# A two-layer decoder trunk on one core: first half of each output product finished in pairs, eight load slots, modulation tiles three ahead

## The chip, the core and the metric

One core of a Trainium2 chip. The time is device microseconds of one execution. The kernel before was run three times: median 2452.31 us, 2449.97 to 2458.36. The engines: TensorE (PE in the profile, its weight loads PEld), VectorE (DVE), ScalarE (ACT), GpSimd (POOL), and SyncE (SP), whose queue issues nearly all loads.

## What is computed

x is one sequence of 256 tokens and 2048 features, c one conditioning vector of 2048. All numbers are float32. Two layers; layer 0 mixes tokens with chunked gated linear attention (GLA), layer 1 with softmax attention that has a forget gate (FoX). Each mixer is followed by a gated MLP with a causal convolution of width 3. Cut to its frame:

```python
cond = jax.nn.silu(c)
for i in range(DEPTH):
    mod = (cond @ w_mod[i] + b_mod[i])[:, None, :]
    sh_m, sc_m, g_m, sh_f, sc_f, g_f = jnp.split(mod, 6, axis=-1)
    h = rmsnorm(x, norm_mix[i]) * (1.0 + sc_m) + sh_m
    y = gla_mixer(h, ...) if i % N_MIXERS == 0 else fox_mixer(h, ...)
    x = x + (1.0 + g_m) * y
    h = rmsnorm(x, norm_ffn[i]) * (1.0 + sc_f) + sh_f
    x = x + (1.0 + g_f) * conv_ffn(h, ffn_w_up[i], ...)
return rmsnorm(x, norm_final)
```

Each mixer ends in a product with w_out (2048 x 2048) and each MLP in a product with ffn_w_down (5632 x 2048). These are the four output products. w_mod (2 x 2048 x 12288) is read once, for one vector: the modulation.

## The kernel before

**Products.** Features lie on the 128 partitions, tokens along the free side. A weight tile is 128 rows by 1024 columns, 512 KB. Each float32 product is made of three matmuls on split operands: weight high by input high, weight high by input low, weight low by input high (lines 612 to 614 in stream_a, 648 to 650 in stream_b, where the weights are the moving operand). ACT makes the high half of a weight tile (wh, line 117), DVE the low half (wl, line 121); there are four buffers of each (AHEAD + 1). stream_a runs over the weight tiles k of one group of 1024 output columns, and for each k over its eight 128-column pieces m: 24 matmuls a tile, added up in four PSUM banks, two pieces to a bank. The pool psA has six banks.

**Loads.** All weight tiles stand in one list (plan) in the order of use. next_w (line 561) hands out the next tile and has split_to (line 571) split up to three tiles beyond it, or fewer where hold says so, and issue loads for up to RING - 1 = 6 tiles beyond those that are split. A load takes one of RING = 7 slots of one pool (ringt, line 100), and is issued on SP's queue; it stays there until a slot is free, and what is behind it stays too.

**Modulation.** mod_tasks (line 236) makes a task for each 128 x 1024 tile of w_mod: a load into a slot of the same ring (line 250), and a product with one column of cond added to an accumulator by DVE (line 271, the first one line 269). At the end of 1024 columns the accumulator is transposed and reduced (lines 283 and 284, or line 304 with line 313) and PE adds up the rest (line 300 or 293). These tasks are spread as background work: after each weight tile tick (line 368) first fills the row of loaded tasks (prefetch, line 350) up to PEND = 2, and then runs as many tasks as pace says; set_pace (line 396) divides the tasks that remain by a number of ticks (N1 = 26 for the last of them in the GLA output product, others for other stages). Small steps of other work (side) are spread in the same way.

**Order.** The instructions are traced in the order of the program. From that a scheduler makes the order of each engine, by what is ready first in its own model of time; so work further on in the program can go ahead on an engine. On the chip each engine then keeps that order. Line 119 and others pin one step behind another.

**Output products.** add_residual (line 678) calls stream_a twice, for columns 0 to 1023 and 1024 to 2047. The first call runs all tiles, and behind it the four residual steps are written, one for each bank: residual (line 667) has two DVE steps that add the scaled bank to x (line 671) and the square for the next norm (stat, lines 454, 462 and 473). The second call gets the residual as done: its last TAIL = 3 tiles are held, without a tick, and then multiplied piece by piece; after each second piece, when a bank is complete, its residual step follows. After the second call come the sum over features for the norm (line 483), what was deferred of the modulation (line 293), and the next h (lines 527 to 530).

Of the kernel before, what the change touches and what calls it, by code (L numbers as in the profile page):

```python
# [28 lines left out]
GH = 4  # L29
FH = 16  # L30
SECT = {"sh_m": 0, "sc_m": 1, "g_m": 2, "sh_f": 3, "sc_f": 4, "g_f": 5}
RING = 7
AHEAD = 3
DIRECT = 4
XAFTER = 1
# [2 lines left out]
BACK = 1  # L38
STAGE = 3
FREE = 0  # L40
PEND = 2
BLOCKS = (8, 8)
FIRST = (6, 0)
SLOW = 0.0
TAIL = 3
# [25 lines left out]
def kernel(  # L71
# [10 lines left out]
    const = ctx.enter_context(tc.tile_pool(name="const", bufs=1))  # L82
    ring = ctx.enter_context(tc.tile_pool(name="ring", bufs=RING))
    big = ctx.enter_context(tc.tile_pool(name="big", bufs=NBIG))
# [15 lines left out]
    def ringt(shape, s="w"):  # L100
        return ring.tile(shape, F32, tag="w", name=nm(s))
# [10 lines left out]
    def split_w(src, moving, after=None):  # L112
        n_ = src.shape[-1]
        o1, o2 = (0, 0) if moving else HELD
        hi = tmp.tile([P, WCOLS], F32R, tag="wh", bufs=AHEAD + 1, name=nm("wh"))[:, o1:o1 + n_]
        lo = tmp.tile([P, WCOLS], F32R, tag="wl", bufs=AHEAD + 1, name=nm("wl"))[:, o2:o2 + n_]
        nc.scalar.copy(out=hi, in_=src)  # L117
        with ExitStack() as es:
            if after is not None:
                es.enter_context(tc.issue_after(after))  # L120
            order["v"] = nc.vector.tensor_tensor(out=lo, in0=src, in1=hi.bitcast(F32), op=ALU.subtract).ins  # L121
        return hi, lo
# [101 lines left out]
    deferred = []  # L224
# [4 lines left out]
    def after_startup(on=True):  # L229
        es = ExitStack()  # L230
        if on and startup["left"] > 0 and len(startup["loads"]) >= BACK:
            startup["left"] -= 1
            es.enter_context(tc.issue_after(startup["loads"][-BACK]))
        return es
# [108 lines left out]
    def modcol(l, key, m):  # L343
        return mod[:, l * 6 + SECT[key], m:m + 1]
# [5 lines left out]
    def prefetch(depth):  # L350
        while bg and len(pending) < depth:
            load, f = bg.popleft()
            load()
            pending.append(f)
# [6 lines left out]
    def flush_resting(all_=False):  # L361

        for r in resting:
            r[0] -= 1
        while resting and (all_ or resting[0][0] <= 0):
            resting.popleft()[1]()

    def tick():
        prefetch(PEND)
        flush_resting()  # L370
        with ExitStack() as es:
            for key in ORDERED:
                if order[key] is not None and fetched["use"] > FREE:
                    es.enter_context(tc.issue_after(order[key]))
            steps()
# [185 lines left out]
    def next_w(kt, cols, hold=None):  # L561
        i = fetched["use"]
        assert plan[i][1] == kt and plan[i][3] == tuple(cols), (plan[i][1:], kt, cols)
        fetched["use"] += 1
        run, look = AHEAD if hold is None else hold, RING - 1
        if i < STAGE:
            run, look = min(run, STAGE - i), 1
        split_to(min(i + 1 + run, len(plan)), look)
        return splits.popleft()

    def split_to(end, look=RING - 1):
        while fetched["split"] < end:
            while fetched["load"] < min(fetched["split"] + look, len(plan)):
                w_, kt_, nk_, cols_, mov_ = plan[fetched["load"]]
                fetched["load"] += 1
                wt = ringt([P, 1024])
                o = 0
                for c0, cn in cols_:
                    if nk_ == 1:
                        with after_startup():  # L580
                            nc.sync.dma_start(out=wt[:, o:o + cn], in_=w_[kt_ * P:(kt_ + 1) * P, c0:c0 + cn])
                        o += cn
                    else:
                        nc.sync.dma_start(out=wt[:, :nk_ * cn].rearrange("p (k r) -> p k r", r=cn),
                                          in_=w_[kt_ * P:(kt_ + nk_) * P, c0:c0 + cn]
                                          .rearrange("(k p) r -> p k r", p=P))
                        nc.vector.memset(wt[:, nk_ * cn:nk_ * cn + P - cn], 0.0)
                        o = nk_ * cn + P - cn
                raws.append((wt[:, :o], mov_))
            with ExitStack() as es:  # L590
                after = None
                if gate["n"] > 0:

                    gate["n"] -= 1
                    es.enter_context(tc.issue_after(gate["early"] if gate["n"] > 0 else gate["late"][0]))
                    after = gate["late"][1]
                splits.append(split_w(*raws.popleft(), after))
            fetched["split"] += 1

    def banks():  # L600
        return [psA.tile([P, 2, T], F32, tag="a", name=nm("pa")) for _ in range(4)]

    def stream_a(kts, cols, rhs, done=None):

        ps = banks()
        held = []

        def mms(m, k, wh, wl, rh, rl):
            first, last = k == kts[0], k == kts[-1]
            ms = slice(m * P, (m + 1) * P)  # L610
            o = ps[m // 2][:, m % 2, :]
            nc.tensor.matmul(o, wh[:, ms], rh, start=(first and m % 2 == 0), stop=False, skip_group_check=True)  # L612
            nc.tensor.matmul(o, wh[:, ms], rl, start=False, stop=False, skip_group_check=True)  # L613
            nc.tensor.matmul(o, wl[:, ms], rh, start=False, stop=last, skip_group_check=True)  # L614

        for k in kts:
            rh, rl = rhs(k)
            tail = done is not None and k in kts[-TAIL:]
            wh, wl = next_w(k, cols, kts[-1] - k + 1 if tail else None)
            if tail:  # L620
                held.append((k, wh, wl, rh, rl))
                continue
            for m in range(8):
                mms(m, k, wh, wl, rh, rl)
            tick()
        if done is not None:
            split_to(min(fetched["use"] + 1, len(plan)))
            if len(deferred) > 1:
                deferred.pop(0)()
            for m in range(8):  # L630
                for args in held:
                    mms(m, *args)
                if m % 2 == 1:
                    done(m // 2, ps)
        return ps
# [31 lines left out]
    def residual(l, key, m0):  # L667
        def done(pair, ps):
            for j in range(2):
                m = m0 + 2 * pair + j  # L670
                nc.vector.scalar_tensor_tensor(out=xT[:, m, :], in0=ps[pair][:, j, :], scalar=modcol(l, key, m),
                                               in1=xT[:, m, :], op0=ALU.mult, op1=ALU.add)
            stat(m0 + 2 * pair, m0 > 0)
            if fin and m0 and 0 < pair < 3:
                transpose_out(m0 + 2 * pair - 2, 2)
        return done

    def add_residual(l, key, kts, rhs):
        ps = stream_a(kts, [(0, 1024)], rhs)
        for pair in range(4):  # L680
            residual(l, key, 0)(pair, ps)
        if l == 1 and key == "g_f":
            prepare_out()
        stream_a(kts, [(1024, 1024)], rhs, residual(l, key, 8))
# [11 lines left out]
    def gla(l, h):  # L696
# [3 lines left out]
        def piece(key, kts, c0):  # L700
            if key == "a":
                return narrow(kts, c0, RANK, h)
            if key[0] == "v":
                return stream_b(kts, c0, h)
            return [p.rearrange("p j t -> p (j t)") for p in stream_a(kts, [(c0, 1024)], h)]
# [469 lines left out]
    def prepare_out():  # L1175
        nfb = bigt([P, D], "nfb")
        nc.sync.dma_start(out=nfb, in_=norm_final.rearrange("(o d) -> o d", o=1).to_broadcast([P, D]))
        fin["g"] = nfb
        fin["o"] = [bigt([P, D], "ot") for _ in range(TT)]
        for m in range(0, 8, 4):  # L1180
            side.append(lambda m=m: transpose_out(m, 4))

    def transpose_out(m, n_):
        for tt in range(TT):
            pt = misc()
            for j in range(n_):
                nc.tensor.transpose(pt[:, j * P:(j + 1) * P], xT[:, m + j, tt * P:(tt + 1) * P], ident)
            cs = slice(m * P, (m + n_) * P)
            nc.vector.tensor_tensor(out=fin["o"][tt][:, cs], in0=pt[:, :n_ * P], in1=fin["g"][:, cs], op=ALU.mult)
# [145 lines left out]
```

## Time and profile before

| | before |
|---|---|
| median of 3 runs | 2452.31 us (2449.97 to 2458.36) |
| profiled execution | 2452.57 us, of which its span is 2450.8 us |
| DVE / ACT busy | 1926.7 us / 1254.9 us |
| split of a weight tile | 1.05 us on ACT (x819), 1.22 us on DVE (x819) |
| modulation product | 1.28 us on DVE (x352) |
| DMA busy, bytes | 76.8% of 16 engines on the main queue; 638.32 MB, mean 260 GB/s |

How to read it: the profile is one execution. A row of a group gives line, engine, operation, result <- operands, shape, count, busy time, mean ns of one, and after the last bar the idle time of the engine just before it, with what ended it. Matmuls overlap, so the mean of one matmul is longer than the time from one to the next; counts in a stretch of time tell PE's rate. A row of waits reads: who waited <- for whom: us in total, times, longest.

### The profile page before, as it was taken

The numbers are of one execution on the slowest core, as the hardware profiler recorded it, in microseconds if no ns is written. First come the engines' busy times: TensorE is split into PE (matmuls) and PEld (weight loads), VectorE is DVE, ScalarE is ACT, GpSimd is POOL, SyncE is SP. The second block draws the span as 40 slices with busy tenths as digits, with TensorE's granted clock in tenths as the row PEclk, the third lists the DMA queues.
The fourth block names the chain that finished last, engine by engine and source line by source line (L and its number), as shares of the span: only waits on it lengthen the run. The fifth ranks groups of instructions, "written<-read, shape, count | busy, mean of one in ns | idle before, by whom it ended". The sixth has DMA issues, their size and how long they took to land.

```text
span 2450.8 us, 46953 instructions
## 1 busy us (share of the span) xinstructions
PE 2401.6 (98%) x19147; PEld 2313.5 (94%) x19150; DVE 1926.7 (79%) x2587; ACT 1254.9 (51%) x1700; POOL 16.5 (1%) x35
## 2 busy tenths in 40 slices
PE   6999999999999999999999999999999999999998
PEld 6998899899999999999988888999999999999998
DVE  7777989887789999987587898887876777777544
ACT  2456555444655555543454545554655555555433
POOL 0000000000000000000000000000000000000000
PEclk7999999899999999999999999999999999999999
DMA  9897878798668888999589887687677777756553
GB/s 371 281 314 239 301 260 313 277 315 313 201 192 273 304 290 307 308 336 320 182 287 311 302 291 235 222 292 250 220 236 233 233 235 237 230 194 220 192 190 112
DMA packets 184309, 638.32 MB, mean 260 GB/s; under 512 B 23961, under 2 KB 24971, under 8 KB 183708
## 3 DMA queue, kind: packets, MB, share of 16 engines
q1 hardware_dynamic: 183128, 634.12, 76.8%
q8 instruction: 150, 2.46, 0.4%
q10 hardware_dynamic: 964, 1.20, 0.1%
q14 instruction: 67, 0.55, 0.1%
HBM read 633.14 MB, written 2.10 MB: 259 GB/s over the span
## 4 chain that ended last, share of the span: by engine, by line
PE 88%; DVE 5%; DMA 5%; issue 1%; ACT 0%; SPq 0%; DVEq 0%; ACTq 0%
PE pa L614 23%; PE pa L613 23%; PE pa L612 23%; PE pa L650 5%; PE pa L649 5%; PE pa L648 5%; DMA wm<-in_w_mod_dram 4%; DVE wl L121 2%; DVE acc L271 1%; PE pm L483 0%; PE pt L293 0%; PE pm L852 0%; DMA w<-in_gla_w_in_dram 0%; PE pm L1063 0%; PE pm L874 0%
## 5 line engine op out<-in xcount | busy, mean ns | idle before, releaser
L117 ACT CAST wh<-w 128x1024 fp32r<-128x1024 f32 x819 | 855.9, 1048 | 985.4 <-PE pa L613 686.2
L121 DVE TENSOR_TENSOR wl<-w,wh 128x1024 fp32r<-128x1024 f32 x819 | 993.4, 1219 | 315.5 <-ACT wh L117 311.3
L613 PE MATMUL pa<-h,wh 128*128 128x256 f32 x3584 | 992.3, 278 | 2.3 <-DVE h L530 2.3
L614 PE MATMUL pa<-h,wl 128*128 128x256 f32 x3584 | 990.8, 278 | 3.5 <-DVE wl L121 3.5
L612 PE MATMUL pa<-h,wh 128*128 128x256 f32 x3584 | 990.6, 278 | 3.3 <-ACT h L528 1.8
L614 PEld LDWEIGHTS pa<-h,wl 128*128 128x128 f32 x3584 | 673.1, 188 | 7.1 <-DVE wl L121 4.5
L613 PEld LDWEIGHTS pa<-h,wh 128*128 128x128 f32 x3584 | 675.5, 189 | 3.3 <-DVE h L530 3.1
L612 PEld LDWEIGHTS pa<-h,wh 128*128 128x128 f32 x3584 | 673.6, 189 | 4.4 <-ACT h L528 2.2
L271 DVE SCALAR_TENSOR_TENSOR acc<-wm,cT,acc 128x1024 f32<-128x1024 f32 x352 | 451.9, 1284 | 131.0 <-DMA wm<-in_w_mod_dram 129.4
L613 PE MATMUL pa<-op,wh 128*128 128x256 f32 x1920 | 527.9, 277 | 0.4 <-DVE op L546 0.4
L612 PE MATMUL pa<-op,wh 128*128 128x256 f32 x1920 | 527.2, 277 | 0.0
L614 PE MATMUL pa<-op,wl 128*128 128x256 f32 x1920 | 523.6, 277 | 0.4 <-DVE wl L121 0.4
L613 PEld LDWEIGHTS pa<-op,wh 128*128 128x128 f32 x1920 | 360.5, 188 | 0.6 <-DVE op L546 0.6
L612 PEld LDWEIGHTS pa<-op,wh 128*128 128x128 f32 x1920 | 359.8, 188 | 0.0
L614 PEld LDWEIGHTS pa<-op,wl 128*128 128x128 f32 x1920 | 357.3, 188 | 0.8 <-DVE wl L121 0.6
L649 PE MATMUL pa<-wh,h 128*128 128x512 f32 x512 | 200.1, 392 | 0.0
L648 PE MATMUL pa<-wh,h 128*128 128x512 f32 x512 | 198.7, 392 | 0.0
L650 PE MATMUL pa<-wl,h 128*128 128x512 f32 x512 | 194.3, 393 | 0.0
L1115 ACT ACTIVATE y<-u,cw 128x256 f32<-128x256 f32 x176 | 101.8, 599 | 30.9 <-DVE act L1131 28.6
L648 PEld LDWEIGHTS pa<-wh,h 128*128 128x128 f32 x512 | 96.2, 188 | 19.3 <-issue 0.2
L650 PEld LDWEIGHTS pa<-wl,h 128*128 128x128 f32 x512 | 95.9, 188 | 19.5 <-DVE wl L121 0.3
L649 PEld LDWEIGHTS pa<-wh,h 128*128 128x128 f32 x512 | 96.2, 188 | 19.1
(258 smaller groups left out, 1350.6 us busy)
## 6 DMA issues: line engine op xcount, KB each, us to landing
wm<-in_w_mod_dram SPq DMA_DIRECT2D x352, 512.0 KB, 5.2
w<-in_ffn_w_up_dram SPq DMA_DIRECT2D x320, 512.0 KB, 4.5
w<-in_ffn_w_down_dram SPq DMA_DIRECT2D x176, 512.0 KB, 4.5
w<-in_fox_w_in_dram SPq DMA_DIRECT2D x128, 512.0 KB, 5.0
w<-in_gla_w_in_dram SPq DMA_DIRECT2D x96, 512.0 KB, 5.1
wm<-in_w_mod_dram SPq DMA_DIRECT2D x16, 1024.0 KB, 12.3
w<-in_gla_w_out_dram SPq DMA_DIRECT2D x32, 512.0 KB, 6.0
w<-in_ffn_w_up_dram SPq DMA_DIRECT2D x64, 256.0 KB, 4.1
```

The source lines that it names most:

```text
L117: nc.scalar.copy(out=hi, in_=src)
L121: order["v"] = nc.vector.tensor_tensor(out=lo, in0=src, in1=hi.bitcast(F32), op=ALU.subtract).ins
L271: nc.vector.scalar_tensor_tensor(out=st["a"], in0=wt[:, j, :], scalar=col, in1=st["a"], op0=ALU.mult, op1=ALU.add)
L612: nc.tensor.matmul(o, wh[:, ms], rh, start=(first and m % 2 == 0), stop=False, skip_group_check=True)
L613: nc.tensor.matmul(o, wh[:, ms], rl, start=False, stop=False, skip_group_check=True)
L614: nc.tensor.matmul(o, wl[:, ms], rh, start=False, stop=last, skip_group_check=True)
L648: nc.tensor.matmul(o, lh[:, ts_], wh[:, hs_], start=first, stop=False)
L649: nc.tensor.matmul(o, ll[:, ts_], wh[:, hs_], start=False, stop=False)
L650: nc.tensor.matmul(o, lh[:, ts_], wl[:, hs_], start=False, stop=last)
L1115: nc.scalar.activation(y, u, AF.Identity, scale=cw[:, l * 3 + 2, r:r + 1], bias=cw[:, 6 + l, r:r + 1])
```

## The change

RING becomes 8; the look-ahead of weight loads, which was RING - 1 = 6, becomes a constant of its own, LOOK = 6. PEND becomes 3. The first half of each output product gets the residual as done too, with two held tiles (TAIL - 1) in place of three; a deferred step of the modulation is taken up before a held tail only in second halves, as before.

```diff
-RING = 7
+RING = 8
+LOOK = 6
...
-PEND = 2
+PEND = 3
...
-        run, look = AHEAD if hold is None else hold, RING - 1
+        run, look = AHEAD if hold is None else hold, LOOK
...
-    def split_to(end, look=RING - 1):
+    def split_to(end, look=LOOK):
...
-    def stream_a(kts, cols, rhs, done=None):
+    def stream_a(kts, cols, rhs, done=None, tail_=TAIL):
...
-            tail = done is not None and k in kts[-TAIL:]
+            tail = done is not None and k in kts[-tail_:]
...
-            if len(deferred) > 1:
+            if len(deferred) > 1 and tail_ == TAIL:
                 deferred.pop(0)()
...
     def add_residual(l, key, kts, rhs):
-        ps = stream_a(kts, [(0, 1024)], rhs)
-        for pair in range(4):
-            residual(l, key, 0)(pair, ps)
+        stream_a(kts, [(0, 1024)], rhs, residual(l, key, 0), TAIL - 1)
         if l == 1 and key == "g_f":
             prepare_out()
         stream_a(kts, [(1024, 1024)], rhs, residual(l, key, 8))
```

## Prediction

> **What bounds the kernel now.** I read the page first, for the busy time of each engine.
>
> ```profile
> span 2450.8 us, 46953 instructions
> PE 2401.6 (98%) x19147; PEld 2313.5 (94%) x19150; DVE 1926.7 (79%) x2587; ACT 1254.9 (51%) x1700; POOL 16.5 (1%) x35
> PEclk7999999899999999999999999999999999999999
> ```
>
> TensorE (PE) is busy in 98% of the span, at nearly full clock. The change adds and removes no matmul and no load, so it can only win time in which PE waits. Second I read the table by stage, five stretches from one answer (the number behind x counts matmuls; the last three numbers are the granted clock, the DMA share and GB/s).
>
> ```profile
> 498.00:618.00 120.00, 114.83 (x1000) 113.68 (x999) 91.70 (x94) 55.88 (x67) 0.00 (x0) 1.00 0.89 314
> 618.00:738.00 120.00, 119.89 (x1056) 119.89 (x1057) 94.72 (x140) 71.89 (x97) 0.00 (x0) 1.00 0.62 196
> 180.00:245.00 65.00, 60.60 (x477) 56.66 (x477) 45.95 (x59) 40.95 (x63) 0.00 (x0) 0.97 0.76 244
> 410.00:466.00 56.00, 52.99 (x468) 52.79 (x466) 52.12 (x60) 26.14 (x44) 0.00 (x0) 1.00 0.99 366
> 850.00:1010.00 160.00, 157.76 (x1377) 156.57 (x1376) 152.24 (x209) 95.99 (x136) 0.00 (x0) 1.00 0.89 304
> ```
>
> Stretch 618 to 738 is PE at its floor: 120 us / 1056 = 0.1136 us a matmul, so one weight tile (24 matmuls) takes 2.73 us. Stretch 498 to 618 does the same kind of work and gets 56 matmuls fewer: 56 x 0.1136 = 6.4 us lost. Stretch 850 to 1010 lacks 160/0.1136 - 1377 = 31, which is 3.5 us. Third, what PE waited for, from 62 us (after the start) to 2440 us (before the last norm):
>
> ```profile
> PE pm L300 <- DVE red L284: 4.0, 4, 1.8
> PE pm L483 <- DVE ss L476: 3.9, 1, 3.9
> PE pa L614 <- DVE wl L121: 3.9, 5, 1.2
> PE pm L304 <- DVE acc L271: 2.8, 1, 2.8
> PE pa L613 <- DVE h L530: 2.3, 4, 1.1
> PE pa L612 <- DVE q L725: 1.5, 1, 1.5
> PE pm L1063 <- ACT pt L1056: 0.6, 1, 0.6
> ```
>
> These come to 19.0 us, nearly all behind VectorE (DVE): PE waits because DVE is late. Fourth, what makes DVE late: the group of modulation products on the page, and DVE's waits from 498 to 618 and from 180 to 245.
>
> ```profile
> L271 DVE SCALAR_TENSOR_TENSOR acc<-wm,cT,acc 128x1024 f32<-128x1024 f32 x352 | 451.9, 1284 | 131.0 <-DMA wm<-in_w_mod_dram 129.4
> DVE acc L271 <- DMA wm<-in_w_mod_dram: 27.8, 21, 2.6
> DVE acc L271 <- DMA wm<-in_w_mod_dram: 14.6, 9, 3.2
> ```
>
> DVE works in order. When a modulation tile (wm) has not landed, DVE stands still, and the low half (wl) of the next weight tile, which PE needs, stands behind it. In the first stage it did so 21 times, 27.8 / 21 = 1.32 us each; nearly all of DVE's idle time there (120 - 91.70 us) is this wait. One such place, in DVE's timeline:
>
> ```profile
> 596.06 1.29 DVE L271 SCALAR_TENSOR_TENSOR acc<-wm,cT,acc 128x1024 f32<-128x1024 f32 x1 [2.65 <-DMA wm<-in_w_mod_dram]
> 597.26 2.36 DVE L121 TENSOR_TENSOR wl<-w,wh 128x1024 fp32r<-128x1024 f32 x2
> ```
>
> **Three tiles ahead and an eighth slot (the part that can win).** The time a wm load takes to land (page, part 6) and the wait of a wm issue on SP's queue for a slot to come free, from 498 to 618:
>
> ```profile
> wm<-in_w_mod_dram SPq DMA_DIRECT2D x352, 512.0 KB, 5.2
> SPq L250 <- DVE wl L121: 21.4, 25, 2.0
> ```
>
> A load needs 5.2 us plus a slot wait of 21.4 / 25 = 0.86 us, 6.1 us in all. In this stage 32 modulation steps are spread over 43 weight tiles (set_pace(48 - 5)), one in 2.73 x 43/32 = 3.67 us. A load is issued at the tick after a step, and its own step is the second from that step: a lead of 2 x 3.67 - 2.73 = 4.6 us. 6.1 - 4.6 = 1.5 us late, near the 1.32 us seen. With three ahead the lead is 3 x 3.67 - 2.73 = 8.3 us, 2.2 us to spare. The eighth slot pays for it: 6 + 2 wanted of 7 before, 6 + 3 of 8 after, so the shortage of one slot stays and weight loads are not pushed back. So I take the waits of this stage as gone. Of the 6.4 us I count 5.5: the two reductions at each end of a modulation chunk stay in DVE's order, and what PE waits for them is partly DVE's own work.
>
> From 180 to 205 the pace is 32/44, the lead 2 x 2.73 x 44/32 - 2.73 = 4.8 us, again under 6.1. There the last product ends a PE wait, and the clock drops behind it:
>
> ```profile
> 196.84 1.28 DVE L271 SCALAR_TENSOR_TENSOR acc<-wm,cT,acc 128x1024 f32<-128x1024 f32 x1 [3.20 <-DMA wm<-in_w_mod_dram]
> 195.00:200.00 5.00, 2.21 (x18) 0.95 0.70 240
> 200.00:205.00 5.00, 5.00 (x34) 0.71 0.85 286
> ```
>
> DVE waited 3.20 us for this tile, PE 2.8 us for DVE (row L304 above): 2.8 us won. The second row is a granted clock of 0.71 over 5 us, which is 2 x 0.29 x 5 = 2.9 us at half speed, 1.4 us lost; whether it goes is not known, so it stands in the low end alone. The Trainium skill, TensorE: Matmul & The Clock Gate, section "What's actually happening", says that the array falls to half its clock after an idle window of about 3.4 us; the rows agree with the half clock, and by that rule the 1.4 us goes with the wait.
>
> From 205 to 245 the pace is 0.95 a tile: a lead of 2 x 2.87 - 2.73 = 3.0 us, with three 5.9 us, about the 6.1 us needed. Of the 1.5 us (row L725) I take 0.8. From 850 to 1010 the pace is 96/151, the lead 2 x 4.29 - 2.73 = 5.9 us, and DVE is busy 152.24 of 160 us: that stage is held by DVE's work, which the change leaves as it is. I take 1.0 of the 3.5 us.
>
> At the start of the first mixer one more 512 KB load goes ahead of weight loads. The fastest short stretch of transfers that I looked at (last number, GB/s):
>
> ```profile
> 440.00:445.00 5.00, 3.41 (x3) 1.00 1.02 416
> ```
>
> At 416 GB/s 524288 B take 1.26 us; bounds 0 to +1.3 us, taken as 0, because weight tiles are split three ahead (8.2 us of cover).
>
> **The first half by pairs (the part that looks large).** It takes four residual steps from behind the last matmul of a first half and puts them beside the last 48. What it could win is what PE loses at the four places where a first half turns into a second:
>
> ```profile
> 415.00:425.00 10.00, 10.00 (x91) 1.00 1.03 399
> 1087.00:1097.00 10.00, 10.00 (x91) 1.00 0.81 279
> 1660.00:1670.00 10.00, 10.00 (x90) 1.00 0.84 292
> 2313.00:2323.00 10.00, 10.00 (x91) 1.00 0.50 172
> 700.00:710.00 10.00, 10.00 (x90) 1.00 0.59 181
> ```
>
> The last row is PE at its floor, the others are equal to it: nothing to win. On its two free banks PE can run 12 matmuls of each of three split tiles before it needs a bank back. What it adds: two of the four split buffers are held for 48 x 0.1136 = 5.5 us, so only one tile of the second half is surely split when the tail ends; the next waits for a buffer that comes free at the tail's start. Its split (1.05 us on ACT, 1.22 us on DVE) then has 5.5 + 2.73 us. If ACT or DVE takes it only behind the last residual instead, it is ready 2 x 0.48 + 0.63 + 1.05 + 1.22 = 3.9 us after the tail against 2.73 us: 1.1 us a place. These rows give the durations:
>
> ```profile
> L121 DVE TENSOR_TENSOR wl<-w,wh 128x1024 fp32r<-128x1024 f32 x819 | 993.4, 1219 | 315.5 <-ACT wh L117 311.3
> L671 DVE SCALAR_TENSOR_TENSOR xT<-pa,mod,xT 128x256 f32<-128x256 f32 x64 | 27.1, 477 | 9.8 <-PE pa L614 9.8
> 457.34 1.05 ACT L117 CAST wh<-w 128x1024 fp32r<-128x1024 f32 x1 [2.04 <-DMA w<-in_ffn_w_up_dram]
> 461.67 0.63 ACT L462 ACTIVATE sq<-xT 128x512 f32<-128x512 f32 x1 [3.27 <-DVE xT L671]
> ```
>
> Bounds 0 to 4 x 1.1 = +4.4 us; I take 0, since the residuals of today's second halves and first halves alike are interleaved with splits.
>
> The held tail also drops two ticks of each first half. In the first mixer's output product there are 16 + 13 = 29 ticks before and 27 after, against a pace set for 26 (N1), so the last modulation steps move from the second half's tile 9 to tile 11. That matters where DVE finishes that product:
>
> ```profile
> 458.42 1.23 DVE L121 TENSOR_TENSOR wl<-w,wh 128x1024 fp32r<-128x1024 f32 x1 [0.66 <-ACT wh L117]
> 459.56 1.28 DVE L271 SCALAR_TENSOR_TENSOR acc<-wm,cT,acc 128x1024 f32<-128x1024 f32 x1
> 460.76 1.65 DVE L671 SCALAR_TENSOR_TENSOR xT<-pa,mod,xT 128x256 f32<-128x256 f32 x4
> ```
>
> The residuals start late behind a wl and an acc, which costs the 3.9 us of row L483. The stage is full of transfers (share 0.99). An earlier first up-projection tile would help by one transfer, 1.26 us; two later products in front of the residuals would cost 2 x 1.28 = 2.6 us. I take 0 between -1.3 and +2.6.
>
> **Sum.** 5.5 + 2.8 + 0.8 + 1.0 = 10.1 us off. The profiled execution took 2452.57 us, its span is 2450.8 us and 1.8 us lie around it; the median of the three runs is 2452.31 us, practically the same. 2452.6 - 10.1 = 2442.5 us.
>
> **Rivals.** (a) The waits only shrink: nine loads still want eight slots, and if the extra modulation load just waits in SP's queue, or transfers are at their ceiling, the stage from 498 to 618 keeps half its loss and the rest half too. Then 5 us are won: 2447.6 us. For it: the shortage of a slot is the same. The stage moves 314 GB/s and would need 1.744 x 524288 B / 2.73 us = 335. Against it: 416 GB/s in the row from 440 to 445. The Trainium skill, DMA: Bandwidth & Descriptors, section "Where 436 GB/s comes from", puts the memory's limit for one core at about 358 GB/s; by that rule the 335 would still fit with 6% to spare and latencies would grow. The trace goes over that figure in short stretches.
>
> (b) Slower: the two dropped ticks. If the last two modulation steps of the first mixer stand in front of its residuals and wait for tiles in a stage full of transfers, as acc did 3.20 us at 196.84, they cost 2 x (1.28 + 3.2) = 9.0 us in front of the norm, for which PE has nothing else to do. It decides once a product lies ahead of the residuals on DVE with its tile not landed. With the 1.1 us at four places, 13.4 us against a gain of 5: 2461 us. For it: an acc lies there already. Against it: that one did not wait, and DVE gets two tiles' time without products before.
>
> (c) The pairs are what counts and the loads nothing: no PE loss at the turns, so 2452 us.
>
> **How the numbers follow.** Forecast 0.5, (a) 0.3, (b) 0.1, (c) 0.1. A measurement of this kernel tells about 0.3% (7.4 us) from no change. The forecast (8 to 17 us off, with the clock and more of the 850 to 1010 stretch) is mostly beyond that, (a) mostly within. Low: 10.1 + 1.4 + 2.5 (the rest of 850 to 1010) + 1.3 + 1.6 (the remainders 0.9 and 0.7 of the first and third terms) = 16.9 off, 2436 us. High: no gain and +4.4 us at the turns, 2457 us; (b) lies outside. Faster 0.52, within 0.38, slower 0.10.
>
> **What would show it.** Right: DVE's waits on wm fall from 129.4 us to under 50; stretch 498 to 618 reaches about 1045 matmuls; the wait of L304 at 195 us is gone; the four turns stay at 90 or 91 in 10 us. Wrong: wm waits as before (then a), the wait of L483 near 460 us longer than 3.9 us with an acc ahead of xT (then b), or new waits of L612 to L614 on wl right after a turn.

## The result and the profile after

The changed kernel takes 2433.98 us (median of 4 runs, 2433.64 to 2434.49), the kernel before in the same sessions 2452.86 us (2449.97 to 2458.36): a ratio of 0.9921, 95% interval 0.9903 to 0.9938, some 19 us faster. The profiled execution took 2434.49 us, its span 2432.8 us. The way was forecast, the size was not: 10.1 us were predicted, and 2434 lies 2 us below the range. (Line numbers of the changed kernel are one higher from line 33 to line 678, and one lower behind that: wl is L122, acc L272.)

DVE's waits on a modulation tile, in the kernel before and then in the changed one (us in total, times, longest):

```profile
DVE acc L271 <- DMA wm<-in_w_mod_dram: 129.4, 111, 3.2
DVE acc L269 <- DMA wm<-in_w_mod_dram: 10.0, 6, 5.0
```

```profile
DVE acc L272 <- DMA wm<-in_w_mod_dram: 5.5, 6, 1.3
DVE acc L270 <- DMA wm<-in_w_mod_dram: 5.1, 2, 5.0
```

139.4 us have become 10.6. What PE waits for from 62 to 2425 us in the changed kernel:

```profile
PE pm L484 <- DVE ss L477: 2.9, 1, 2.9
PE pa L614 <- DVE h L531: 2.6, 4, 1.1
PE pa L615 <- DVE wl L122: 1.2, 1, 1.2
PE pm L1053 <- issue: 0.6, 1, 0.6
PE pm L1062 <- DVE mx L1041: 0.6, 1, 0.6
PE pm L664 <- DVE h L531: 0.4, 1, 0.4
PE pm L519 <- issue: 0.2, 1, 0.2
```

The reductions (L300), the transposes of acc (L304) and q (L725) are gone from the list; what is left is mostly the norm and the first h. By stage, with the borders put at the same matmuls in both kernels, first before, then after (length; busy time of PE, PEld, DVE, ACT, POOL; granted clock, DMA share, GB/s):

```profile
498.90:621.70 122.80, 117.52 (x1023) 116.37 (x1022) 94.50 (x102) 59.58 (x73) 0.00 (x0) 1.00 0.89 311
180.30:244.10 63.80, 59.40 (x467) 55.46 (x466) 44.75 (x58) 39.77 (x62) 0.00 (x0) 0.97 0.76 245
409.10:479.90 70.80, 66.66 (x522) 63.68 (x522) 60.23 (x77) 31.74 (x52) 0.00 (x0) 0.90 0.82 300
849.70:1011.00 161.30, 159.06 (x1389) 157.87 (x1388) 153.54 (x211) 96.93 (x136) 0.00 (x0) 1.00 0.89 302
```

```profile
490.40:607.10 116.70, 116.48 (x1027) 116.28 (x1027) 95.01 (x100) 59.25 (x73) 0.00 (x0) 1.00 0.92 328
179.70:236.60 56.90, 56.79 (x467) 53.45 (x466) 42.65 (x56) 38.63 (x60) 0.00 (x0) 1.00 0.79 263
401.30:471.20 69.90, 66.75 (x523) 63.77 (x523) 59.62 (x76) 31.63 (x52) 0.00 (x0) 0.90 0.82 304
835.00:992.20 157.20, 157.20 (x1388) 157.20 (x1387) 153.57 (x213) 97.57 (x136) 0.00 (x0) 1.00 0.90 311
```

The first, second and fourth stage give 6.1, 6.9 and 4.1 us, 17.1 of the 18.0 that the spans differ by. In the fourth, PE is now busy the whole time beside the same DVE work (153.57 us, before 153.54). The four turns from a first half to a second stay where they were, at PE's floor (the row of a turn gives its length, PE's busy time and matmuls, granted clock, DMA share, GB/s):

```profile
406.00:416.00 10.00, 10.00 (x91) 1.00 0.99 362
1069.00:1079.00 10.00, 10.00 (x91) 1.00 0.67 225
1641.00:1651.00 10.00, 10.00 (x90) 1.00 0.66 255
2295.00:2305.00 10.00, 10.00 (x91) 1.00 0.50 165
```

Why a third tile or an eighth slot could do so much is in the chain of waits of the kernel before, in the stage from 498 to 618. First the shares by line from 521 to 564 us, then pieces of it (start, us, what; pieces left out are marked):

```profile
by line: DMA wm<-in_w_mod_dram 59.4%; DVE wl L121 22.2%; issue 11.8%; DVE acc L271 6.6%; DVE red L284 2.1%; DVE acc L269 1.7%; DVE mt L283 1.7%; DVE mod L321 1.3%; DVEq L121 0.3%; DVEq L271 0.2%; DVE mod L327 0.1%
...
521.41 1.23 DVE wl L121
522.63 0.02 issue
522.65 5.22 DMA wm<-in_w_mod_dram
...
527.97 0.09 DVE acc L271
528.05 1.11 issue
529.17 1.23 DVE wl L121
530.41 5.13 DMA wm<-in_w_mod_dram
...
536.84 1.23 DVE wl L121
538.08 4.91 DMA wm<-in_w_mod_dram
```

It is a loop, and PE is not in it: from 521 to 612 us the chain goes through modulation loads, DVE and short issue times alone. A modulation load is issued when a wl frees a slot; it lands 5.2 us later; acc runs as soon as it lands; behind acc stands the next wl; that frees the slot for the load after the next. Two tiles are in flight, so each round carries two. From 522.65 to 538.08 are two rounds of 7.7 us, 3.86 us a tile, where the pace wants one every 3.67 us.

Some of the rounds behind them are longer. From the acc at 527.97 to the twentieth behind it, at 607.84, it is 79.9 us, 3.99 us a tile. The same twenty steps take 73.7 us in the changed kernel (517.60 to 591.29), 3.68 us a tile, which is the pace. The difference is 6.2 us, and the stage lost 6.1.

### The profile page after: what moved, and what is told of

The parts are those of the page before. It is cut to its first block, busy times and chain, and to the rows that moved or that the text cites. A ratio compares the mean times of both kernels' runs of the same rounds, so it can differ in the third digit from the quotient of the medians.

```text
span 2432.8 us, 46933 instructions
## 1 busy us (share of the span) xinstructions
PE 2394.7 (98%) x19147; PEld 2309.5 (95%) x19150; DVE 1929.0 (79%) x2587; ACT 1255.9 (52%) x1700; POOL 17.1 (1%) x35
## 4 chain that ended last, share of the span: by engine, by line
PE 96%; DVE 2%; DMA 1%; issue 0%; ACT 0%; SPq 0%; DVEq 0%
PE pa L615 26%; PE pa L614 26%; PE pa L613 25%; PE pa L650 5%; PE pa L651 5%; PE pa L649 5%; DMA wm<-in_w_mod_dram 1%; DVE acc L272 1%; PE pm L484 0%; PE pt L294 0%; DVE wl L122 0%; PE pm L851 0%; PE pm L873 0%; PE pm L1062 0%; PE pm L1008 0%
## 5 line engine op out<-in xcount | busy, mean ns | idle before, releaser
L122 DVE TENSOR_TENSOR wl<-w,wh 128x1024 fp32r<-128x1024 f32 x819 | 996.3, 1218 | 417.0 <-ACT wh L118 412.4
L272 DVE SCALAR_TENSOR_TENSOR acc<-wm,cT,acc 128x1024 f32<-128x1024 f32 x352 | 450.2, 1279 | 6.2 <-DMA wm<-in_w_mod_dram 5.5
```

What stands on the lines that cost most here:

```text
L272: nc.vector.scalar_tensor_tensor(out=st["a"], in0=wt[:, j, :], scalar=col, in1=st["a"], op0=ALU.mult, op1=ALU.add)
```

## The experiments

Theory L was that modulation tiles land too late and the change brings them in time; P, that the pairs carry a share. Later theories are named in the expectations. Where a run's time is given by stage, the borders are the same matmuls in each trace.

**One part of the change each.** The kernel without the pairs:

```diff
-        stream_a(kts, [(0, 1024)], rhs, residual(l, key, 0), TAIL - 1)
+        ps = stream_a(kts, [(0, 1024)], rhs)
+        for pair in range(4):
+            residual(l, key, 0)(pair, ps)
```

> Eight slots, three modulation tiles ahead, first halves finished as before the change. Theory L (the gain is modulation tiles landing before VectorE wants them): 17 to 19 us faster than the kernel before, so within 1 us of the changed kernel; VectorE's waits on wm near the 10.6 us of the changed kernel. Theory P (the pairs carry a share): the share is missing, at least 2 us of the 18.

2433.20 us, ratio to the kernel before 0.9921 (0.9908 to 0.9933), waits on wm 10.8 us. The pairs alone (RING = 7, PEND = 2):

> Seven slots, two tiles ahead, first halves finished by pairs from two held tiles. Theory L: within 2 us of the kernel before, the same waits on wm (about 140 us). Theory P: at least 2 us faster. The slower rival of the prediction (the two dropped ticks push modulation products in front of the residuals near 460 us): 3 to 9 us slower, with a longer wait of the norm's sum on VectorE than 3.9 us.

2452.39 us, ratio 0.9997 (0.9988 to 1.0006), waits 132.0 us, and the norm's sum waits 3.8 us. The pairs do nothing that can be measured here to within some 2 us, alone or with the rest, and the dropped ticks do not cost the 3 to 9 us of the slower rival.

The slot alone (the first kernel with PEND = 2), and the third tile alone (the first kernel with RING = 7):

> Eight slots, two tiles ahead, no pairs. Theory L by leads: the lead stays 4.6 us from 498 to 618 and only the slot wait (0.86 us) goes, so the lateness falls from 1.5 to about 0.6 us and about half of the gain comes, 6 to 11 us; waits on wm 40 to 80 us. Theory S (the slot alone does it, since what was short was room for loads of any kind): 16 to 19 us faster, waits on wm under 20 us.

> Seven slots, three tiles ahead, no pairs: nine loads want seven slots. Theory L by leads: the third tile's load stands in SP's queue for a slot, and weight loads stand behind it; 0 to 8 us faster, waits on wm 60 to 120 us, and more waits of wh on its load than before. Theory S: within 2 us of the kernel before, waits on wm as before. A third outcome, the lead alone being enough: 16 to 19 us faster.

2436.47 us, ratio 0.9933 (0.9920 to 0.9945), waits 38.7 us; and 2437.62 us, ratio 0.9940 (0.9926 to 0.9953), waits 21.4 us. By the medians the slot alone brings 16.8 us and the third tile alone 15.6. The second is the third outcome, but for 0.4 us; the first has the gain of theory S with more waits than it allowed. My working by leads, half for the slot and at most 8 us for the third tile, falls. One part of it came: with the third tile alone ScalarE waits 59.5 us for weight loads, before 48.2, but of that only 1.0 us reaches PE. By stage both are at the floor or within 1 us of it:

| us from matmul to matmul | 180-245 | 498-622 | 850-1011 | waits on wm | a tile, the twenty steps |
|---|---|---|---|---|---|
| before | 63.8 | 122.8 | 161.3 | 139.4 | 3.99 |
| changed | 56.9 | 116.7 | 157.2 | 10.6 | 3.68 |
| pairs alone | 64.1 | 124.2 | 160.2 | 132.0 | 3.99 |
| slot alone | 56.9 | 116.8 | 157.2 | 38.7 | 3.67 |
| third tile alone | 57.9 | 116.3 | 157.2 | 21.4 | 3.68 |

In the stage from 498 to 622 the twenty steps take either the pace or 3.99 us. That is what a loop does: it sets the time when its round is longer than the pace allows, and otherwise costs nothing.

The loop is shown for that stage alone. From 850 to 1010 the pace is 4.29 us, longer than the 3.86 us of those rounds, and the chain there goes mostly through PE: wm loads have 8.0% of it, among them two that took 6.5 and 6.4 us, at 876 and 889 us. That the loads landed late there is shown, what made them late is not. From 180 to 205 it was one wait at a chunk's end, 2.8 us, and the clock behind it.

**Is it room, or what is asked of it?** With the slot alone, eight loads are wanted (6 + 2) of eight slots. Two runs separate one more load in flight from the end of the shortage: LOOK = 7 with eight slots, and LOOK = 5 with seven slots, both with PEND = 2 and no pairs.

> Eight slots, weights looked ahead 7 in place of 6, two modulation tiles, no pairs: the eighth slot is spent on weight loads, nine loads want eight slots. Theory R (the run with the slot alone was fast because its eight loads had eight slots, so a modulation load no longer stood behind a weight load that had no slot): waits on wm back at 100 us or more, 0 to 5 us faster than the kernel before. Theory F (one more load in flight, of whatever kind, is what counts): as the slot alone, 15 to 18 us faster, waits on wm under 50 us.

> Seven slots as before, weights looked ahead 5 in place of 6, two modulation tiles, no pairs: seven loads want seven slots, no memory is added. Theory R: 14 to 18 us faster than the kernel before, waits on wm 30 to 60 us. Theory F: within 2 us of the kernel before, waits on wm about 130 us.

2450.53 us, ratio 0.9999 (0.9984 to 1.0013); and 2438.95 us, ratio 0.9949 (0.9934 to 0.9964). Their waits on wm, and what their wm issues waited for on SP's queue in the stage from 498 to 618, first with LOOK = 7, then with LOOK = 5:

```profile
DVE acc L272 <- DMA wm<-in_w_mod_dram: 131.3, 113, 5.0
SPq L251 <- DVE wl L122: 21.0, 24, 2.0
```

```profile
DVE acc L272 <- DMA wm<-in_w_mod_dram: 34.4, 35, 2.7
SPq L251 <- DVE acc L272: 24.1, 25, 1.4
```

Theory R holds, F falls, though the gain with LOOK = 5 is 12.5 us where R said 14 to 18. A slot that is given to weight loads brings nothing (the twenty steps take 4.00 us each); one weight load fewer in the same seven slots brings some 12 us and takes no memory (3.68 us each). The rows show the link that changes: nine wanted of eight, and a modulation load is released by a wl, which stands behind an acc that waits; seven of seven, and an acc releases it, one step earlier in DVE's order. That makes the round shorter by a wl: an estimate from the rows above is (7.7 - 1.2) / 2 = 3.2 us a tile, under the pace. The changed kernel gets there in the other way. Its loads still wait for a wl (from 490 to 607 us):

```profile
SPq L251 <- DVE wl L122: 31.6, 27, 2.0
```

But three tiles share a round: 7.7 / 3 = 2.6 us a tile by the same estimate.

Both at once, five weights ahead and three tiles, with eight slots and with seven (there four weights ahead):

> Eight slots, weights 5 ahead, three modulation tiles, no pairs: eight loads want eight slots, and a lead of three. Theory R: waits on wm under 10 us, and since the lead alone and the slot alone each leave little, 18 to 21 us faster than the kernel before, within 2 us of eight slots and three ahead without pairs. Theory F: the same. It is the candidate for the fastest.

> Seven slots as before, weights 4 ahead, three modulation tiles, no pairs: seven loads want seven slots, with the lead of three and no added memory. Theory R: waits on wm under 20 us and 14 to 20 us faster than the kernel before. Theory F (one more load in flight is what counts): within 2 us of the kernel before. A third outcome: weights only 4 ahead land too late, TensorE waits for wl or wh in the stage full of transfers (410 to 466 us), 5 to 12 us faster.

2433.91 us, ratio 0.9928 (0.9912 to 0.9944), waits 8.3 us (17.6 us faster by the medians, just short of the 18 expected); and 2434.48 us, ratio 0.9930 (0.9911 to 0.9950), waits 8.2 us. The second has the memory of the kernel before and the time of the changed one. Weights four ahead are not late for PE: its only waits on their halves are 1.2 us on wl and 0.9 on wh.

**Does VectorE's work hold a stage?** I had left 2.5 of the 3.5 us of the stage from 850 to 1010 to DVE's work. Two runs add work where no load is late (on the kernel without pairs; the added line stands in split_w, and TWICE gives 1 for chosen tiles, else 0), and one takes work away from the kernel before.

```diff
             order["v"] = nc.vector.tensor_tensor(out=lo, in0=src, in1=hi.bitcast(F32), op=ALU.subtract).ins
+            for _ in range(TWICE(fetched["split"])):
+                order["v"] = nc.vector.tensor_tensor(out=lo, in0=src, in1=hi.bitcast(F32), op=ALU.subtract).ins
```

> The kernel without pairs (eight slots, three ahead), with the low half of a weight tile computed a second time on VectorE, to the same values: for 16 of the tiles of the stage from 500 to 617 us and for 8 of the tiles of the stage from 850 to 1010. Theory B (a stage loses what VectorE's work and waits together exceed TensorE's own time of 116.7 and 157.2 us): the first stage has 93.9 us of work, 16 x 1.22 = 19.5 more make 113.4, nothing lost (0 to 1 us); the second has 153.6 us, 8 x 1.22 = 9.8 more make 163.4, 6 us lost. Theory C (work on VectorE is hidden as long as no load is late): nothing lost in either.

> The same with 32 tiles of the first stage and 3 of the second. Theory B: 93.9 + 39.0 = 132.9 us of work against 116.7, 16 us lost in the first stage (14 to 18); 153.6 + 3.7 = 157.3 against 157.2, nothing lost in the second (0 to 1 us). Theory C: nothing lost in either.

The medians are 2439.54 us, ratio 0.9945 (0.9925 to 0.9964), and 2449.61 us, ratio 0.9984 (0.9973 to 0.9995). The two stages of the first run, then of the second:

```profile
487.30:604.10 116.80, 116.58 (x1028) 116.38 (x1027) 111.80 (x116) 59.21 (x73) 0.00 (x0) 1.00 0.93 328
832.00:994.30 162.30, 158.84 (x1389) 157.79 (x1388) 160.70 (x219) 97.54 (x136) 0.00 (x0) 1.00 0.87 296
```

```profile
489.60:622.80 133.20, 123.89 (x1026) 120.69 (x1025) 130.71 (x139) 61.46 (x75) 0.00 (x0) 0.97 0.85 288
850.90:1008.10 157.20, 157.20 (x1389) 157.20 (x1388) 155.11 (x214) 96.95 (x136) 0.00 (x0) 1.00 0.88 306
```

0, 5.1, 16.5 and 0 us lost, where theory B said 0, 6, 16 and 0 and theory C nothing at all. With loads in time a stage costs about what DVE's work exceeds PE's time by: by the busy times of the rows 3.5 and 14.0 us, so 1.6 and 2.5 us less than was lost. In the third row the granted clock of 0.97 may have a part in that. At 153.6 of 157.2 us the stage from 850 to 1010 has 3.6 us of room. Then work taken away: the kernel before without the third tap of the convolution in layer 0.

```diff
-            nc.vector.scalar_tensor_tensor(out=y[:, 2:], in0=u[:, :T - 2], scalar=cw[:, l * 3, r:r + 1],
-                                           in1=y[:, 2:], op0=ALU.mult, op1=ALU.add)
+            if l > 0:
+                nc.vector.scalar_tensor_tensor(out=y[:, 2:], in0=u[:, :T - 2], scalar=cw[:, l * 3, r:r + 1],
+                                               in1=y[:, 2:], op0=ALU.mult, op1=ALU.add)
```

> The kernel before with seven slots and two tiles ahead; the third tap of the convolution is left out in layer 0, which takes about 35 x 0.48 = 16.7 us of work off VectorE in the stage from 850 to 1010 us and nothing off any load. Theory B (work and waits together against 157.2 us): 153.6 - 16.7 = 136.9 us of work and 7.4 us of waits, or a few more, stay under 157.2: the 4.1 us that the stage lost are gone, the waits on wm are not; the stage from 500 to 617 still loses about 6 us. Theory D (a wait on wm costs TensorE time by itself): the stage still loses 3 us or more.

2453.37 us, ratio 0.9994 (0.9981 to 1.0008); the stage:

```profile
853.90:1013.90 160.00, 157.85 (x1386) 157.26 (x1385) 142.56 (x179) 95.63 (x134) 0.00 (x0) 1.00 0.89 303
```

DVE is busy 11.0 us less, and the stage still takes 160.0 us with two matmuls fewer in it, some 3 us over the floor: theory D's 3 us or more, at its edge. The waits on wm have grown from 7.4 to 14.3 us in place of the work. So theory B does not hold where slots are short: a wait there is no fixed amount that free time absorbs. That a DVE that is done earlier only waits longer for the same tile fits this, but was not followed tile by tile. How much of the remaining 3 us is late loads and how much is bunched work was not taken apart.

**The two dropped ticks.** The changed kernel was 1.3 us behind the one without pairs after the first output product, in one profile of each. The changed kernel with N1 = 24 in place of 26:

> The changed kernel with the modulation of the first output product paced for 24 ticks in place of 26, which gives back the two ticks that the held tail takes. If the dropped ticks are why the changed kernel is 1.3 us behind the one without pairs after that product: 0.5 to 2 us faster than the changed kernel (2432 to 2433.5 us), the norm's sum waiting 2.3 us or less near 450 us. If not: within 0.5 us of it.

2432.36 us (2429.11 to 2433.22), ratio 0.9919 (0.9903 to 0.9935). The median is 1.6 us lower and the norm's sum waits 2.3 us, as the first outcome has it, but the intervals of the two ratios cannot tell the kernels apart. Its profiled execution is 5.4 us shorter than the changed kernel's, nearly all of it behind that product, and the clock shows why that says little. The stretches after the norm, of the changed kernel, of this one, and of the kernel without pairs (PE busy, granted clock, DMA share, GB/s):

```profile
460.00:465.00 5.00, 5.00 (x20) 0.50 0.04 13
465.00:470.00 5.00, 4.76 (x18) 0.50 0.00 0
```

```profile
460.00:465.00 5.00, 5.00 (x41) 1.00 0.00 0
465.00:470.00 5.00, 4.92 (x44) 1.00 0.87 273
```

```profile
455.00:460.00 5.00, 2.72 (x14) 0.89 1.05 253
460.00:465.00 5.00, 5.00 (x27) 0.77 0.10 39
```

The first goes through the restart at half clock, the second at full clock, with 38 against 85 matmuls in 10 us. The third has the same wait in front of it as the second, 2.3 us, and part of it is at half clock. Inconclusive: whether the ticks matter stays open below about 2 us.

## Why the prediction was right in direction and wrong in size

- **What bounds the kernel** was read rightly: PE at its floor but for places where DVE is late, and DVE late through wm. The waits on wm fell to 10.6 us, under the 50 us forecast; the stage from 498 to 618 reached PE's floor.
- **The pairs at nothing**: right to within 2 us, by the turns and by the run with the pairs alone. Rival (c) had it the wrong way round. Rival (b), two products in front of the residuals, did not come: the norm's sum waits 2.9 us, before 3.9.
- **The leads** gave the right sign, but not the cause, so their fair lateness (1.5 us against 1.32) was luck. "The eighth slot pays for it" supposed that the third tile needs the slot; either does it alone, and so does asking for one load fewer. What I took for a tile that starts too late was, from 498 to 618, a loop of two tiles, 3.99 us a tile over twenty steps against a pace of 3.67.
- **The step that failed** is the sum: the mechanism, late modulation tiles, was right, and three of its four terms were far too small. Its terms and what they measured (from matmul to matmul): 498 to 618, 5.5 for 6.1; 180 to 205, 2.8 for 4.9; 205 to 245, 0.8 for 2.0; 850 to 1010, 1.0 for 4.1. The last is the largest miss: "that stage is held by DVE's work, which the change leaves as it is". The work is unchanged and the stage is at PE's floor. The numbers that say so stood in the prediction: 152.24 us of work are less than the 160 - 3.5 = 156.5 us that PE needs at its floor, so the work alone cannot make the stage longer. The run with the third tap left out says the same: with 11.0 us less of DVE's busy time and the loads still late, the stage stays some 3 us over its floor. Even all that the prediction had counted as lost in these stretches, 6.4 + 2.8 + 1.5 + 3.5 us and 1.4 of clock, is 15.6 us, against 17.1 measured.
- **The clock** behind the wait at 195 us was left to the low end. It went with the wait. In the prediction's two rows the half clock is 3.4 us long, 0.5 of them in the first row, so it cost 1.7 us; with the 2.8 us of the wait that is 4.5 of the 4.9 us. In the changed kernel:

```profile
195.00:200.00 5.00, 5.00 (x47) 1.00 0.50 157
200.00:205.00 5.00, 4.89 (x43) 1.00 0.34 105
```

0.71 has become 1.00, and 18 + 34 matmuls in these 10 us have become 47 + 43. The Trainium skill, TensorE: Matmul & The Clock Gate, section "What's actually happening", has the half clock follow an idle window of about 3.4 us, and the windows run free of the program. The half clock went with the wait, as that has it, but the wait was 2.8 us, shorter than the page's window. Free-running windows would also explain why a wait of 2.3 us at the same norm had half clock behind it in one execution and none in another, which the runs show without showing why.

- Rival (a), half of each wait left, was built on "nine loads still want eight slots". They do, and it cost nothing.

The Trainium skill, Perfetto Trace Analysis, section "Identifying Performance Opportunities", says that a gap that repeats on the engine which should be full can mean that there is not enough memory for the next tile. The run with the slot alone agrees (16.8 us). The run with five weights ahead in seven slots shows another way out: 12.5 us with the same memory. Here more was wanted than there was, and either side could give.

## What to carry to other kernels

When several streams of loads share one ring of slots and one in-order queue, add up what the look-aheads ask for before adding memory. With more wanted than slots, a load of the stream with the fewest tiles ahead can end up waiting for a slot that is freed behind its own consumer. The round of that loop, divided by its tiles in flight, is then a floor of its own. Follow several rounds in the chain of waits, take the mean over many, and compare it with the pace that the consumer needs; here the whole excess was the gain, whichever link was cut. For a sum of gains, take the stage's time less the busy engine's floor, not the waits that the engine's list names, and leave no part of it to another engine whose work fits into the floor.

## What the runs showed of the hardware that was not expected

After the norm near 460 us the array's clock was at half for two 5 us stretches in one profile and at full in another of nearly the same program, worth some 5 us of one execution: a single profile of this kernel is no measure of differences under 0.2%. The length of the wait does not decide it: after 2.3 us the granted clock was 0.89 and 0.77 in the 5 us stretches of one run, and 1.00 in those of another. Loads ran at 416 GB/s from 440 to 445 us of the kernel before, while PE was busy for all of the 5 us.
